# A hybrid HGRN2 / stick-breaking transformer block in float32: the low part of the output projections' moving operand by a subtraction on VectorE, and the feed-forward's sums moved from GpSimd to VectorE

## The chip, the cores and the metric

One core of one Trainium2 chip runs the whole block as one launch. The metric is device microseconds of that core. The kernel before took 2149.41 us, the median of 3 runs (2149.28 to 2149.68). The engines are called by the names of the profile: PE is TensorE (PEld its weight loads), DVE is VectorE, ACT is ScalarE, POOL is GpSimd, SP is SyncE, which here only issues DMAs.

## What is computed

A transformer block of depth 1 on a sequence of 1024 tokens and a width of 1024, in float32. The parts that this change touches are the three output projections and the feed-forward. Cut to what matters:

```python
y_hg = o_hg @ w_hg_out                         # 1024 x 1024 @ 1024 x 1024
y_sb = o_sb @ w_sb_out
mixed = sigmoid(ga) * y_hg + sigmoid(gb) * y_sb
x = x + mixed @ w_o
h2 = rms_norm(x, norm2_gain)
gate, up = split_cols(h2 @ w_ffn_in, (2816, 2816))
x = x + (silu(gate) * up) @ w_ffn_out
```

Ahead of them lie a norm, the input projections, the HGRN2 mixer and the stick-breaking attention. They fill about the first 1200 us of the span.

## The kernel before

**Numbers in two parts.** TensorE multiplies a rounded form of float32 (`F32R`). To keep float32 accuracy, each operand is split into a high part, `hi`, which is the operand rounded to `F32R`, and a low part, `lo = raw - hi`. A product is three matmuls into one PSUM bank: hi*hi, hi*lo and lo*hi (`mm3`, L140 to L144). So each operand costs, besides its load, a cast on ACT (`hi`) and a subtraction (`lo`).

There are two helpers for the low part. `split` (L875 to L877) casts on ACT at L876 and subtracts on an engine that is handed to it, at L877. `rest_by_dma` (L106 to L109) instead lets ACT write the negated high part into `lo` (L107), and then lets POOL issue a DMA that adds `raw` to it on the way (L108, `accum_op=add`).

**Seven products for eight.** The three output projections, and the two products of the feed-forward, use a scheme of seven block products `m` = 1 to 7 in place of the eight of a 2 x 2 partition (four quarters of A, four of B). Some of the seven take a sum or difference of quarters as an operand; `sum_step` (L870 to L873) makes it in place in the raw tiles. The quarters have the numbers 11, 12, 21 and 22. The products are summed in four PSUM banks per chain, and partial results are taken out after each product.

**Output projections** (`Product`, L887 to L943). A phase is one projection, of seven jobs, one for each `m`; there are 21 jobs, `job_steps(0)` to `job_steps(20)`. A job is 4 tiles of 4 steps of 3 matmuls of 128 x 512, 48 in all. While it runs, `prep` of the job after it is woven in, in four parts: `moving(0)`, `moving(1)`, `stationary(0)` and `stationary(1)`. The stationary side is summed by `sum_step` at L873 and split by `split`, on DVE, in two halves of 1024 elements a partition. The moving side is summed on DVE, cast on ACT (L925), and its low part comes by `rest_by_dma` (L926), also in two halves of 1024 elements. The raw quarters of the job two ahead are loaded on SP.

After each tile, partial results leave PSUM: `accumulate` copies them on ACT (L953) or adds them on DVE (L951). Where a result is final, `gated` loads the gate's values from DRAM into one of three `m` tiles (L977, SP), takes the sigmoid on ACT (L978) and multiplies on DVE (L979); in the second phase DVE also adds the first phase's result (L986). In the third phase DVE adds each tile to `x` (L991).

**Feed-forward in.** The last job of the projections is woven with `turn_h2`, which multiplies by the norm (L1068, DVE), transposes on PE (L1072), and splits the moving operands `bop[1]`, `[2]`, `[5]`, `[6]` and `[7]` piece by piece (`b_op`, on DVE). The operands for `m` = 3 and 4 are made later by `b_rest` (L1098), four pieces of 128 x 512 each, and these go through `rest_by_dma`. Then 22 column blocks `f` follow, each of seven units of 12 matmuls (`ffn_step`). Their order is the list `a_order`; `a_prep(n)` (L1123 on) makes the stationary operand of the unit `n`, up to five units ahead of the matmuls. For n up to 22 its sum and its subtraction are on DVE. For later ones the sum is on POOL, and so is the subtraction of `m` = 5, 6, 7 and 3; those of `m` = 1, 2 and 4 are on DVE. DVE also takes the results out (L1192, L1171, L1178, L1180).

**Feed-forward out.** Seven products of 11 groups of 12 matmuls (`ffn_out`); `o_tile` makes both operands of a group, up to three groups ahead, on DVE. While `m` = 1 and 2 run, POOL makes the sums that the moving operand of `m` = 5 and 7 will need, 22 of 128 x 512.

**What sets the order.** PE's order is that of the code. On the other engines the tile framework places the instructions by its own estimate of time, so they do not stand in the order of the code. Each engine then runs its instructions strictly in turn, and so does SP's queue of DMA issues; each instruction waits for the ones that it depends on, and those behind it wait too.

Of the kernel before, what the change touches and what calls it, by code (L numbers as in the profile page):

```python
# [34 lines left out]
def hybrid_block(ctx, tc, x, norm1_gain, w_in, lb_logits, hg_out_norm, sb_q_norm, sb_k_norm,  # L35
                 w_hg_out, w_sb_out, w_o, norm2_gain, w_ffn_in, w_ffn_out,
                 c_ident, c_blk, c_lvl, c_base, out):
    nc = tc.nc
# [848 lines left out]
    class Product:  # L887
# [17 lines left out]
        def prep(self, i):  # L905
            m = self.seq[i]
            sides = self.ops[i] = [], []

            def stationary(c):
                cols = slice(c * 256, (c + 1) * 256)  # L910
                raw = lambda q: self.raw("a", q)[:, :, cols]
                hi = wp.tile([P, 4, 256], F32R, tag="wh", name="wh")
                lo = wp.tile([P, 4, 256], F32R, tag="wl", name="wl")
                sides[0].append((hi, lo))
                sum_step(self.a_sum, A_STEPS, m, raw)
                split(nc.vector, raw(A_SRC[m]), hi, lo)

            def moving(c):
                if c == 0:
                    sides[1].extend((unit1(), unit1()))  # L920
                ks = slice(2 * c, 2 * c + 2)
                raw = lambda q: self.raw("b", q)[:, ks, :]
                sum_step(nc.vector, B_STEPS, m, raw)
                hi, lo = (u[:, ks, :] for u in sides[1])
                nc.scalar.copy(hi, raw(B_SRC[m]))  # L925
                rest_by_dma(lo, raw(B_SRC[m]))  # L926
            return [lambda: moving(0), lambda: moving(1), lambda: stationary(0), lambda: stationary(1)]

        def tile(self, i, j):
# [153 lines left out]
    bop = {}  # L1083

    def b_op(m, cut, e):
# [2 lines left out]
            bop[m] = [unit() for _ in range(2)]  # L1088
        raw = lambda q: h2f[q][cut]
        sum_step(e, B_STEPS, m, raw)  # L1090
        if cut[2:]:
            split(e, raw(B_SRC[m]), *(u[cut] for u in bop[m]))
        else:
            hi, lo = (u[cut] for u in bop[m])
            nc.scalar.copy(hi, raw(B_SRC[m]))
            rest_by_dma(lo, raw(B_SRC[m]))

    def b_rest(m, e):  # L1098
        for q in range(4):
# [23 lines left out]
    def a_prep(n):  # L1123
# [4 lines left out]
            load_raw(f + 1)  # L1128
        raw = lambda q: raws[f][q // 10 - 1][:, 4 * (q % 10) - 4:4 * (q % 10), :]
        both = wp.tile([P, 2, 4, P], F32R, tag=("wh", "wl")[n % 2], name="wh")  # L1130
        sum_step(nc.gpsimd if n > 22 else nc.vector, A_STEPS, m, raw)
        split(nc.vector if m in (1, 2, 4) or n <= 22 else nc.gpsimd, raw(A_SRC[m]), both[:, 0], both[:, 1])
        a_ops[f, m] = both

    a_done = []
# [79 lines left out]
    def o_tile(m, g):  # L1215
        def load():
# [7 lines left out]
            split(nc.vector, A(A_SRC[m]), hi[:, 0], lo[:, 0])  # L1224
            split(nc.vector, B(B_SRC[m]), hi[:, 1], lo[:, 1])
            if m in (1, 2):
                sum_step(nc.gpsimd, B_STEPS, {1: 5, 2: 7}[m], B)
            return hi, lo
        return load

# [111 lines left out]
```

## Time and profile before

| | |
|---|---|
| median of 3 runs | 2149.41 us (2149.28 to 2149.68) |
| the profiled execution's own time | 2149.9 us |
| its span, first to last instruction | 2148.1 us |
| mean granted TensorE clock | 0.989 |
| busy in the span: PE, DVE, ACT, POOL | 95%, 63%, 53%, 26% |
| output projections, first matmul of job 0 to first of job 20 | 1213.4 to 1473.5 us, 260.1 us |
| job 20 woven with the transposes, and the start of the feed-forward | 1473.5 to 1552.3 us, 78.8 us |
| feed-forward in, the steady part | 1552.3 to 1920.3 us, 368.0 us |
| feed-forward out | 1920.3 to 2148.1 us, 227.8 us |

In the profile's rows a line number is that of the kernel, `out<-in` are tile names without their buffer numbers, and the shape is partitions x elements. `u` is the name of all large tiles of these stages, raw or split; `wh` and `wl` are the high and low parts of the stationary side; `wr` are raw weights; `pd`, `pt`, `pz` and `po` are PSUM banks. In a row of idle time, `<-` names the engine and line that ended the wait.

### The profile page before, as it was taken

How to read it: one execution, taken by the hardware profiler on the slowest of the kernel's cores; microseconds unless marked ns; L12 is line 12 of the kernel's file. 1: busy time of each engine (PE TensorE's matmuls, PEld its weight loads, DVE VectorE, ACT ScalarE, POOL GpSimd, SP SyncE). 2: the span in 40 equal slices, each digit the busy share in tenths (PEclk: the TensorE clock that was granted, in tenths of full speed). 3: DMA queues.
4: the chain of work that ended last, by engine and by line, in shares of the span. 5: the costliest groups of instructions: out<-in, count | busy, mean ns of one | idle time of the engine just before them, and what ended most of it. 6: DMA issues, size and time to landing. Idle time of an engine off the chain costs nothing.

```text
span 2148.1 us, 29624 instructions
## 1 busy us (share of the span) xinstructions
PE 2045.9 (95%) x10981; PEld 1730.3 (81%) x10981; DVE 1364.0 (63%) x2130; ACT 1143.5 (53%) x1879; POOL 559.0 (26%) x610
## 2 busy tenths in 40 slices
PE   7999999999999999999999998989899999999999
PEld 6889898988877877877887776767688888887887
DVE  6475757656387787788778356678733333337965
ACT  4454554453476776767767365666533333333443
POOL 4333323232221122022020011110255555545000
PEclk9999999999999999999999999999999999999999
DMA  4433334335534434344343779982512322255221
GB/s 147 110 87 94 94 81 115 74 97 135 134 86 105 95 89 115 83 103 103 84 112 101 242 190 263 252 171 99 127 60 79 103 79 75 63 180 210 76 101 46
DMA packets 203840, 250.47 MB, mean 117 GB/s; under 512 B 11256, under 2 KB 134576, under 8 KB 203696
## 3 DMA queue, kind: packets, MB, share of 16 engines
q1 hardware_dynamic: 179552, 183.43, 27.4%
q0 software_dynamic: 16848, 59.25, 14.7%
q10 hardware_dynamic: 7296, 5.90, 0.8%
q8 instruction: 86, 1.41, 0.3%
q14 instruction: 58, 0.48, 0.1%
HBM read 134.51 MB, written 38.01 MB: 80 GB/s over the span
## 4 chain that ended last, share of the span: by engine, by line
PE 67%; DVE 15%; DMA 7%; ACT 6%; issue 4%; POOL 0%; SPq 0%; DVEq 0%; ACTq 0%; POOLq 0%
PE pd L142 15%; PE pd L143 15%; PE pd L144 15%; DVE kp L737 3%; PE pt L144 2%; PE pt L142 2%; PE pt L143 2%; PE pt L770 2%; DMA u<-u 2%; DVE a L744 2%; DVE wl L877 1%; PE pz L507 1%; PE po L142 1%; PE po L787 1%; PE po L144 1%
## 5 line engine op out<-in xcount | busy, mean ns | idle before, releaser
L142 PE MATMUL pd<-hT,wh 128*128 128x512 f32 (+1 forms) x920 | 375.9, 409 | 0.0
L143 PE MATMUL pd<-hT,wh 128*128 128x512 f32 (+1 forms) x920 | 356.4, 387 | 0.5 <-DVE hT L192 0.5
L144 PE MATMUL pd<-hT,wl 128*128 128x512 f32 (+1 forms) x920 | 356.4, 387 | 0.0
L876 ACT CAST wh<-u 128x512 fp32r<-128x512 f32 (+1 forms) x280 | 183.6, 684 | 224.5 <-PE po L144 70.5
L877 DVE TENSOR_TENSOR wl<-u,wh 128x512 fp32r<-128x512 f32 (+1 forms) x196 | 164.1, 873 | 85.0 <-ACT wh L876 82.8
L143 PE MATMUL pd<-u,wh 128*128 128x512 f32 x496 | 197.5, 398 | 12.7 <-DMA u<-u 10.5
L142 PE MATMUL pd<-u,wh 128*128 128x512 f32 x496 | 198.0, 399 | 10.3 <-ACT wh L876 5.5
L144 PEld LDWEIGHTS pd<-hT,wl 128*128 128x128 f32 x920 | 174.2, 189 | 36.3
L143 PEld LDWEIGHTS pd<-hT,wh 128*128 128x128 f32 x920 | 175.5, 191 | 21.4 <-DVE hT L192 0.8
L142 PEld LDWEIGHTS pd<-hT,wh 128*128 128x128 f32 x920 | 175.4, 191 | 21.1
L737 DVE TENSOR_TENSOR_SCAN kp<-kp,dsel 128x512 f32<-128x512 f32 (+3 forms) x128 | 129.5, 1012 | 39.9 <-ACT kp L730 39.9
L142 PE MATMUL pd<-wh,hT 128*128 128x256 f32 x512 | 148.0, 289 | 0.0
L730 ACT ACTIVATE kp<-pz,rq 128x128 f32<-128x128 f32 (+2 forms) x192 | 112.9, 588 | 61.3 <-PE pz L726 52.7
L144 PE MATMUL pd<-wh,hT 128*128 128x256 f32 x512 | 144.8, 283 | 0.0
L143 PE MATMUL pd<-wl,hT 128*128 128x256 f32 x512 | 144.7, 283 | 0.0
L108 POOL DMA_DIRECT2D wl<-wr x67 | 59.0, 880 | 312.6 <-ACT wl L107 240.6
L144 PE MATMUL pd<-u,wh 128*128 128x512 f32 x352 | 138.4, 393 | 0.0
L873 DVE TENSOR_TENSOR u<-u,u 128x512 f32<-128x512 f32 (+1 forms) x130 | 110.3, 883 | 42.7 <-DMA u<-u 13.1
L143 PEld LDWEIGHTS pd<-u,wh 128*128 128x128 f32 x496 | 95.4, 192 | 35.7 <-issue 6.3
L142 PEld LDWEIGHTS pd<-u,wh 128*128 128x128 f32 x496 | 95.4, 192 | 31.7 <-ACT wh L876 6.4
L744 DVE TENSOR_TENSOR a<-a,kp 128x128 f32<-128x128 f32 (+2 forms) x192 | 109.5, 571 | 14.0
L730 ACT ACTIVATE a<-pz,rq 128x128 f32<-128x128 f32 (+2 forms) x192 | 112.8, 587 | 2.7 <-PE pt L770 2.7
(270 smaller groups left out, 5036.7 us busy)
## 6 DMA issues: line engine op xcount, KB each, us to landing
wr<-in_w_in SPq DMA_DIRECT2D x72, 512.0 KB, 3.7
wl<-wr POOLq DMA_DIRECT2D x67, 512.0 KB, 4.6
u<-u POOLq DMA_DIRECT2D x42, 512.0 KB, 7.4
u<-in_w_ffn_in SPq DMA_DIRECT2D x24, 512.0 KB, 5.2
wr<-in_w_ffn_in SPq DMA_DIRECT2D x20, 512.0 KB, 3.7
u<-in_w_ffn_out SPq DMA_DIRECT2D x10, 1024.0 KB, 5.1
d_act<-c SPq DMA_DIRECT2D x33, 256.0 KB, 2.1
u<-d_act SPq DMA_DIRECT2D x8, 1024.0 KB
```

The lines of the kernel that those rows point to most:

```text
L108: nc.gpsimd.dma_start(lo.bitcast(F32).rearrange("p k n -> p (k n)"), raw.rearrange("p k n -> p (k n)"), accum_op=ALU.add)
L142: nc.tensor.matmul(ps, lh, rh, start=start, stop=False, skip_group_check=adds)
L143: nc.tensor.matmul(ps, lh, rl, start=False, stop=False, skip_group_check=adds)
L144: nc.tensor.matmul(ps, ll, rh, start=False, stop=stop, skip_group_check=adds)
L507: nc.tensor.matmul(ps[:, sl], kq[:, 0, sl], kq[:, 1, sl], start=True, stop=True)
L730: last["sig"] = [nc.scalar.activation(t[:, 0:w], ps[:, 0:w], AF.Sigmoid, scale=rq[:, n_, col:col + 1]) for n_, t in enumerate((kp, a))]
L737: nc.vector.tensor_tensor_scan(rev, rev, dsel[:, HS - w:][:, ::-1], initial=0.0, op0=ALU.mult, op1=ALU.max)
L744: nc.vector.tensor_mul(a[:, 0:w], a[:, 0:w], kp[:, 1:w + 1])
L770: nc.tensor.transpose(tp[:, s * P:(s + 1) * P], a[:, b * P:(b + 1) * P], ident)
L873: e.tensor_tensor(raw(to), raw(a), raw(b), op=op)
L876: nc.scalar.copy(hi, src)
L877: e.tensor_sub(lo, src, hi.bitcast(F32))
```

## The change

```diff
 # Product.prep, moving(c): output projections
                 hi, lo = (u[:, ks, :] for u in sides[1])
-                nc.scalar.copy(hi, raw(B_SRC[m]))
-                rest_by_dma(lo, raw(B_SRC[m]))
+                split(nc.vector, raw(B_SRC[m]), hi, lo)
 # b_op: moving operands of the feed-forward
-        if cut[2:]:
-            split(e, raw(B_SRC[m]), *(u[cut] for u in bop[m]))
-        else:
-            hi, lo = (u[cut] for u in bop[m])
-            nc.scalar.copy(hi, raw(B_SRC[m]))
-            rest_by_dma(lo, raw(B_SRC[m]))
+        split(e, raw(B_SRC[m]), *(u[cut] for u in bop[m]))
 # a_prep: stationary operands of the feed-forward
-        sum_step(nc.gpsimd if n > 22 else nc.vector, A_STEPS, m, raw)
-        split(nc.vector if m in (1, 2, 4) or n <= 22 else nc.gpsimd, raw(A_SRC[m]), both[:, 0], both[:, 1])
+        sum_step(nc.vector, A_STEPS, m, raw)
+        split(nc.vector, raw(A_SRC[m]), both[:, 0], both[:, 1])
 # o_tile: second product of the feed-forward
             if m in (1, 2):
-                sum_step(nc.gpsimd, B_STEPS, {1: 5, 2: 7}[m], B)
+                sum_step(nc.vector, B_STEPS, {1: 5, 2: 7}[m], B)
```

In the output projections, 42 negations on ACT and 42 adding DMAs that POOL issues (512 KB each) become 42 subtractions on DVE (128 x 1024). The same happens to 8 pieces of 128 x 512 of the feed-forward's moving operand. In the feed-forward 76 sums and 76 subtractions of 128 x 512 move from POOL to DVE in the first product, and 22 sums in the second. The arithmetic is the same, and so is PE's order of work. The input projections, ahead of all this, go on using `rest_by_dma`.

Since the framework places the work of DVE, ACT and POOL, the order there changes. Two places are shown.

The first is DVE at the start of the first projection. `u1_12221`, `u1_12367` and `u1_12449` (after: `u1_12221`, `u1_12365`, `u1_12445`) are the raw quarters 11, 12 and 22 of the moving side, `wl_12416` (after `wl_12412`) is a low part of the stationary side of job 1. Before:

```order
L873 TENSOR_TENSOR u1_12221<-u1_12367,u1_12221 128x1024 [waits DMAHW5_49,DMAHW4_49,DMAHW7_49,DMAHW0_49,DMASW4_49]
L877 TENSOR_TENSOR wl_12416<-u1_12249,wh_12415 128x1024 [waits DMASW7_49,DMAHW7_49,PE_49,Activation_49]
L873 TENSOR_TENSOR u1_12372<-u1_12372,u1_12374 128x4x256 [waits DMAHW7_49,DMAHW6_49]
L873 TENSOR_TENSOR u1_12372<-u1_12372,u1_12374 128x4x256
L873 TENSOR_TENSOR u1_12367<-u1_12449,u1_12367 128x1024 [waits DMAHW2_49,DMAHW1_49,DVE_49]
L877 TENSOR_TENSOR wl_12433<-u1_12249,wh_12432 128x1024 [waits PE_49,Activation_49]
L873 TENSOR_TENSOR u1_12367<-u1_12449,u1_12367 128x1024 [waits DMAHW4_49,DMAHW3_49,DVE_49]
L951 TENSOR_TENSOR u2_12397<-u2_12397,pt_12460 128x512 [waits PE_49]
```

And after (L950 is the L951 of before):

```order
L873 TENSOR_TENSOR u1_12221<-u1_12365,u1_12221 128x1024 [waits DMAHW5_49,DMAHW4_49,DVE_49]
L877 TENSOR_TENSOR wl_12412<-u1_12247,wh_12411 128x1024 [waits DMASW7_49,DMAHW7_49,PE_49,Activation_49]
L877 TENSOR_TENSOR u1_12375<-u1_12242,u1_12374 128x1024 [waits DMAHW3_49,Activation_49]
L877 TENSOR_TENSOR u1_12375<-u1_12242,u1_12374 128x1024 [waits DMAHW6_49,Activation_49]
L873 TENSOR_TENSOR u1_12370<-u1_12370,u1_12372 128x4x256 [waits DMAHW7_49,DMAHW6_49]
L877 TENSOR_TENSOR wl_12429<-u1_12247,wh_12428 128x1024 [waits PE_49,Activation_49]
L873 TENSOR_TENSOR u1_12370<-u1_12370,u1_12372 128x4x256
L873 TENSOR_TENSOR u1_12365<-u1_12445,u1_12365 128x1024 [waits DMAHW2_49,DMAHW1_49,DVE_49]
L873 TENSOR_TENSOR u1_12365<-u1_12445,u1_12365 128x1024 [waits DMAHW4_49,DMAHW3_49,DVE_49]
L877 TENSOR_TENSOR u1_12451<-u1_12221,u1_12450 128x1024 [waits PE_49,Activation_49]
L873 TENSOR_TENSOR u1_12221<-u1_12445,u1_12221 128x1024 [waits DVE_49]
L950 TENSOR_TENSOR u2_12394<-u2_12394,pt_12455 128x512 [waits PE_49]
```

What moved: the subtractions of the moving side (`u1_12375` for job 1, `u1_12451` for job 2) now stand among the sums and the stationary side's subtractions, and the first sum no longer waits for an adding DMA (DMASW4).

The second place is the start of the feed-forward's steady part. Before, POOL has there the last of `b_rest`'s adding DMAs (`u2_14568`, for `m` = 4), then the sums for `m` = 5 of the column blocks 4, 5, 7 and 9 (`wr_14714`, `u1_14851`, `u1_15119`, `u1_15387`), each of which waits for its block's load, and behind them the work on block 3 (`u1_14287`):

```order
L873 TENSOR_TENSOR wr_14714<-wr_14714 128x512 [waits DMAHW5_49]
L108 DMA u2_14568<-u1_14115 128x512 [waits DMASW2_49,DVE_49,Activation_49]
L108 DMA u2_14568<-u1_14115 128x512 [waits DMASW3_49,DVE_49,Activation_49]
L108 DMA u2_14568<-u1_14115 128x512 [waits DMASW4_49,DVE_49,Activation_49]
L873 TENSOR_TENSOR u1_14851<-u1_14851 128x512 [waits DMASW6_49,DMASW7_49,DMASW5_49,DMAHW7_49,DMASW0_49,PE_49]
L873 TENSOR_TENSOR u1_15119<-u1_15119 128x512 [waits DMAHW1_49]
L873 TENSOR_TENSOR u1_15387<-u1_15387 128x512 [waits DMASW4_49,DMASW3_49,DMAHW3_49,DMASW2_49,DMASW1_49]
L877 TENSOR_TENSOR wh_14773<-u1_14287,wh_14773 128x512 [waits DVE_49,PE_49,Activation_49]
```

After, the same sums stand on DVE (blocks 4, 5, 7 and 9 are now `wr_14664`, `u1_14801`, `u1_15069` and `u1_15337`), and the first result of column block 1 to leave PSUM (L1186, the L1192 of before) stands behind them:

```order
L877 TENSOR_TENSOR wh_14628<-u1_14245,wh_14628 128x512 [waits DMAHW6_49,PE_49,Activation_49]
L873 TENSOR_TENSOR u2_14236<-u2_14236 128x512
L873 TENSOR_TENSOR wr_14664<-wr_14664 128x512 [waits DMAHW6_49]
L873 TENSOR_TENSOR u1_14801<-u1_14801 128x512 [waits DMAHW7_49]
L877 TENSOR_TENSOR wh_14646<-u2_14236,wh_14646 128x512 [waits PE_49,Activation_49]
L873 TENSOR_TENSOR u1_15069<-u1_15069 128x512 [waits DMAHW1_49]
L873 TENSOR_TENSOR u1_15337<-u1_15337 128x512 [waits DMAHW3_49]
L1186 TENSOR_TENSOR c_14552<-c_14552,pd_14349 128x512 [waits PE_49]
```

What moved: four sums that wait for loads, and on which nothing close by depends, have come from POOL's queue into DVE's, between the split of a unit and the taking out of a result.

## The prediction

> **What bounds the kernel now.** I read the page first, then the busy times by stage, then what PE waited for in the stages that the change touches, then DVE, ACT, POOL and the DMA queues there.
>
> ```profile
> span 2148.1 us, 29624 instructions
> PE 2045.9 (95%) x10981; PEld 1730.3 (81%) x10981; DVE 1364.0 (63%) x2130; ACT 1143.5 (53%) x1879; POOL 559.0 (26%) x610
> ```
>
> The 63% of DVE is an average. By stage (length, then busy time and instructions of PE, PEld, DVE, ACT and POOL, granted clock, DMA share, GB/s): output projections, their join to the feed-forward, feed-forward in, feed-forward out; and the projections again from 1231 us on.
>
> ```profile
> 1213.40:1473.50 260.10, 232.31 (x962) 186.41 (x961) 165.92 (x196) 155.70 (x204) 34.68 (x40) 0.94 0.79 210
> 1473.50:1552.30 78.80, 67.37 (x303) 53.57 (x302) 63.58 (x121) 52.18 (x108) 14.70 (x13) 0.91 0.52 136
> 1552.30:1920.30 368.00, 368.00 (x1624) 304.51 (x1622) 134.81 (x196) 136.98 (x231) 195.72 (x148) 1.00 0.27 86
> 1920.30:2148.10 227.80, 219.98 (x961) 179.50 (x960) 169.66 (x251) 87.57 (x154) 32.62 (x22) 1.00 0.33 115
> 1231.00:1473.50 242.50, 218.51 (x905) 175.63 (x905) 159.54 (x191) 147.88 (x194) 32.95 (x38) 0.94 0.77 200
> ```
>
> Feed-forward in is PE alone: 1624 matmuls in 368.00 us, with no idle time, 0.2266 us each. That is the pace of an unhindered PE. The 20 jobs of the projections, 960 matmuls, would take 217.5 us at it and took 260.1, so 42.6 us are lost there: 27.8 of idle time (260.10 - 232.31), and 14.8 of slower matmuls. These follow the gaps:
>
> ```profile
> 1258.76 0.59 PE L143 MATMUL pd<-u,wh 128*128 128x512 f32 x1 [3.56 <-DMA u<-u]
> 1259.15 0.63 PE L144 MATMUL pd<-u,wl 128*128 128x512 f32 x1
> 1259.57 0.63 PE L142 MATMUL pd<-u,wh 128*128 128x512 f32 x1
> ```
>
> After a gap of 3.56 us matmuls start every 0.42 us. PE waits for several things, of which the adding DMAs (`u<-u`) are the largest group; first the projections, then the join:
>
> ```profile
> PE pd L142 <- ACT wh L876: 5.5, 2, 4.7
> PE pd L143 <- DMA u<-u: 5.1, 2, 3.6
> PE pt L143 <- DMA u<-u: 4.1, 3, 2.3
> ...
> PE pd L143 <- DMA u<-u: 5.4, 3, 3.8
> PE pt L1072 <- DVE hn L1068: 3.8, 1, 3.8
> ```
>
> What lies behind the rest is seen in the DMA queues of the projections (packets, MB, share of 16 engines), and in ACT:
>
> ```profile
> q0 software_dynamic: 5760, 20.97, 42.0%
> q1 hardware_dynamic: 19152, 33.16, 36.8%
> u<-u POOLq DMA_DIRECT2D x40, 512.0 KB, 7.2
> ...
> L107 ACT ACTIVATE u<-u 128x1024 fp32r<-128x1024 f32 x40 | 42.1, 1058 | 0.0
> L978 ACT ACTIVATE m<-m 128x512 f32<-128x512 f32 x32 | 19.6, 629 | 60.2 <-DMA m<-d_ga 30.8 <-DMA m<-d_gb 29.3
> ```
>
> The adding DMAs take 42.0% of the DMA engines, more than all plain loads and stores (36.8%), and land 7.2 us after issue. ACT waits 60.2 us for gate tiles on those same engines, and with it the casts queued behind.
>
> **The change, part by part.** First the price of a subtraction on DVE, from runs of the same instruction back to back:
>
> ```profile
> 1252.90 5.76 DVE L873 TENSOR_TENSOR u<-u,u 128x1024 f32<-128x1024 f32 x5
> 1517.56 2.50 DVE L877 TENSOR_TENSOR u<-u,u 128x512 fp32r<-128x512 f32 x4
> ```
>
> So 1.15 us for 1024 elements, 0.625 for 512.
>
> *Projections.* Removed in this stage: 40 negations (42.1 us of ACT), 40 issues on POOL and 42.0% of the DMA engines. A moving low part used to come 1.06 us of ACT plus 7.2 us of DMA after the cast; it will come one DVE slot after it. Added: 40 subtractions on DVE. Two of them fall ahead of 1231 us, where DVE mostly waits for the first loads (`d_ohg`, `in_w_hg_out` below); I leave those waits as they are. From 1231 us on DVE has 159.5 us of work and gets 38 x 1.15 = 43.7 more: 203.2. Without a wait it would be through at 1434.2, 39.3 us sooner than 1473.5. PE needs the sum of 217.5 us from 1213.4, 1430.9. So the two engines come out alike, and what counts is which of DVE's waits stay:
>
> ```profile
> DVE wl L877 <- ACT wh L876: 32.7, 14, 4.9
> DVE u L979 <- ACT m L978: 13.1, 3, 5.8
> DVE u L873 <- DMA u<-u: 13.1, 4, 4.8
> DVE u L873 <- DMA u<-d_ohg: 12.0, 3, 9.3
> DVE u L873 <- DMA u<-in_w_ffn_in: 7.6, 1, 7.6
> DVE u L873 <- DMA u<-in_w_hg_out: 6.0, 1, 6.0
> DVE u L873 <- DMA u<-d_osb: 5.5, 2, 3.2
> ```
>
> The 13.1 for `u<-u` go. The waits for ACT, gate tiles and other loads (32.7 + 13.1 + 7.6 + 5.5 = 58.9) shrink, since ACT loses 42 of 156 us and the DMA engines over half their load; by how much no row shows. Bounds: none stays (gain 39.3); all stay, which is a rival below. I take a quarter, 15 us, nearer to none, because a DVE that runs late finds its casts done. Gain 39.3 - 15 = 24.3. Queued behind a late DVE are the results that free PSUM banks (L951, L991) and the gate multiplications that free the `m` tiles, so PE does feel it.
>
> Of the Trainium skill, Trace Analysis, section Optimizing Scalar/DVE Operations, speaks against this edit: with a saturated DVE, some work may go to Scalar or GPSIMD, and here it comes back. No run so far shows DVE saturated for long; what it would give is the third rival.
>
> *Join.* Eight subtractions of 512 come to DVE (8 x 0.625 = 5.0), and up to five of POOL's sums (3.1): 63.6 + 8.1 = 71.7 of 78.8 us. PE's 5.4 us of waits for the adding DMAs go, with slow matmuls behind them. So 7.1 is the most that DVE allows; if it delays the transposes' inputs as now (3.8), the gain could be lost or turn to -3. I take 5.
>
> *Feed-forward in.* 152 instructions move; POOL needs 195.72 us for 148 of them in this stage, DVE 148 x 0.625 = 92.5. DVE goes from 134.8 to 227.3 of 368 us, 62%. It now idles ahead of each result:
>
> ```profile
> 1709.39 0.69 DVE L877 TENSOR_TENSOR wh<-wr,wh 128x512 fp32r<-128x512 f32 x1 [3.23 <-ACT wh L876]
> 1716.36 0.69 DVE L1192 TENSOR_TENSOR c<-c,pd 128x512 f32<-128x512 f32 x1 [6.28 <-PE pd L144]
> ```
>
> A unit is 12 x 0.2266 = 2.72 us, and operands are made up to five units ahead, 13.6 us. I cost this at nothing, up or down: PE has nothing to gain. The cover goes if a sum on DVE waits for its load for longer than the two units (5.4 us) after which PE returns to the same bank. POOL's queue has such waits, harmless there:
>
> ```profile
> 1540.37 1.28 POOL L873 TENSOR_TENSOR u<-u 128x512 f32<-128x512 f32 x1 [5.32 <-DMA u<-in_w_ffn_in]
> ```
>
> *Feed-forward out.* Twenty-two sums move. While POOL made them, DVE's own instructions were slow, and PE waited:
>
> ```profile
> 1943.79 20.23 DVE L877 TENSOR_TENSOR wl<-u,wh 128x512 fp32r<-128x512 f32 x12 [1.42 <-ACT wh L876]
> ...
> 1941.85 26.30 POOL L873 TENSOR_TENSOR u<-u,u 128x512 f32<-128x512 f32 x16 [0.70 <-DMA u<-in_w_ffn_out]
> ...
> 1968.75 0.50 PE L143 MATMUL pt<-wl,wh 128*128 128x512 f32 x1 [1.66 <-DVE wl L877]
> 1955.00:1975.00 20.00, 17.24 (x72) 12.99 (x71) 17.40 (x18) 6.56 (x13) 12.91 (x8) 1.00 0.21 67
> ```
>
> Twelve splits took 1.69 us each beside POOL, against 0.625 alone. With the sums on DVE two splits and one or two sums make 1.9 to 2.5 us per group of 2.72. In the last row 72 matmuls stand where 88 fit, 3.6 us lost. I take 3 back, between 0 and 4.5. The Trainium skill, SBUF — State Buffer, section Who interferes with whom, says that DVE and GpSimd lock one another out of a shared port pair; the trace agrees, 12 x (0.625 + 1.28) = 23 against 20.23 us.
>
> *Sum.* 24.3 + 5 + 0 + 3 = 32.3. The profiled execution's own time is 2149.9, 1.8 over its span and 0.5 over the median of 2149.41. Taken from the median, 2117.
>
> **The rivals.** *PE sets the pace throughout* (0.12): no wait of DVE stays, 39.3 + 7.1 + 4.5 = 50.9, 2098.5. For it: the DMA share halves. Against: DVE then has no idle microsecond for 200 us, and it depends on ACT at every split.
>
> *DVE becomes the bound, and most waits stay* (0.16): 35 of 58.9, gain 4 in the projections and 2 each in join and output: 2141. For it: 32.7 us are handshakes with ACT, which an engine that works in turn meets at each new subtraction too.
>
> *DVE carries all its waits along* (0.07), the slower end: after 1231 us it idles 242.5 - 159.5 = 83.0; less 13.1, 69.9 stay. Then 1231 + 203.2 + 69.9 = 1504.1, 30.6 later than now, 2180. It decides from 39.3 us of remaining waits. Against: many of those waits are for DMAs that shared the engines with the transfers removed, or for PE, which is late itself.
>
> *Waits of the hoisted sums stop DVE in the feed-forward* (0.05): two waits like POOL's 5.32 cost PE up to 10.6, so 2128 with the rest as forecast. Against: these loads start earlier when no adding DMA holds their buffers.
>
> That the change does nothing has no room: the DMAs are gone from the queue.
>
> **How the numbers follow.** The forecast, 2117, has 0.60; with waits of 3 to 28 us it spans 2105 to 2130. The range from 2097 to 2139 takes in the first and last rivals and leaves out most of the second and all of the third. A difference of 0.2%, 4.3 us, is about what a measurement of this kernel can tell from none. Slower: 0.07, the third rival. Same: 0.03, the second rival's edge. Faster: 0.90.
>
> **What would show it.** Right: no L107 or L108 row on `u`, and the 20.97 MB of q0 in the projections gone; the stretch of jobs 0 to 19 some 24 us shorter, with DVE over 85% busy in it; DMA share near 0.4, and ACT's wait for `m` well under 60.2; feed-forward in still 0.2266 us a matmul; the splits beside the sums of the second product at 0.6 to 0.7 us. Wrong: a gain without a DVE near its limit (first rival), PE waits for DVE in the place of those for DMAs that sum to 25 us or more (second and third), or a DVE L873 that waits for `in_w_ffn_in` with PE idle behind it (fourth).

## The result

The changed kernel takes 2092.7 us (median of 4 runs, 2091.42 to 2094.44) against 2149.35 us before (4 runs, 2143.7 to 2149.68): ratio 0.9743, 95% interval 0.9725 to 0.9761. That is faster by 57 us. Of all the executions below, two ran at a granted clock of 0.56 and 0.66 and took 3362 and 2878 us, one with a late low part and one with VectorE past its limit, and the ratios leave them out. The forecast was 2117 with a range from 2097 to 2139, so the sign was right and the size was not: 32 us were forecast, and the time lies 4 us below the range. The profile of the changed kernel, its page's first lines:

```profile
span 2091.1 us, 29348 instructions
PE 2026.5 (97%) x10981; PEld 1723.8 (82%) x10981; DVE 1508.6 (72%) x2354; ACT 1103.1 (53%) x1829; POOL 280.3 (13%) x386
```

The busy times by stage, in the columns of the prediction: output projections, join, feed-forward in, feed-forward out.

```profile
1212.40:1430.00 217.60, 217.60 (x961) 180.24 (x960) 206.63 (x236) 122.06 (x165) 0.00 (x0) 1.00 0.42 146
1430.00:1500.60 70.60, 64.60 (x304) 52.96 (x303) 69.12 (x133) 48.61 (x100) 0.00 (x0) 0.95 0.40 121
1500.60:1868.60 368.00, 367.77 (x1623) 304.20 (x1621) 230.75 (x344) 135.25 (x232) 0.00 (x0) 1.00 0.27 86
1868.60:2091.10 222.50, 218.42 (x960) 179.90 (x960) 168.61 (x272) 87.46 (x154) 0.00 (x0) 1.00 0.33 118
```

In the projections PE is busy for the whole of 217.60 us at full clock, with VectorE at 95%. What VectorE and ScalarE still wait for there, and the DMA queue (us in total, times, longest; packets, MB, share):

```profile
DVE u L877 <- ACT u L876: 3.2, 5, 1.4
DVE wl L877 <- ACT wh L876: 2.5, 5, 0.9
DVE u L873 <- DMA u<-d_osb: 2.0, 1, 2.0
...
ACT m L977 <- DMA m<-d_gb: 20.5, 10, 3.9
...
ACT m L977 <- DMA m<-d_ga: 13.8, 8, 3.4
...
q1 hardware_dynamic: 18080, 31.18, 41.6%
```

PE has no wait at all in this stretch. VectorE's 32.7 us for `wh` have become 2.5, the 13.1 for gate tiles are gone, and ScalarE's 60.2 us for gate tiles are 34.3.

To compare kernels, the table below takes the times between the same matmuls of the program, counted from the first of the output projections: number 0, 960 (the last job), 1008 (the feed-forward's first), 1164 (its unit 13), and the first of the second product. Each row is of one profiled execution.

| kernel | median us | jobs 0 to 19 | job 20 | units 0 to 12 | units 13 on | second product |
|---|---|---|---|---|---|---|
| before | 2149.35 | 260.1 | 14.6 | 56.7 | 384.5 | 218.8 |
| changed | 2092.7 | 217.6 | 14.6 | 48.2 | 384.5 | 213.8 |

The difference is 42.5 + 0 + 8.5 + 0 + 5.0, and 1.0 in front of the projections, which the change doesn't touch: 57.0 us of span. Every job of the twenty takes 10.88 us now.

### The profile page after: what moved, and what is told of

It is laid out like the page before. It is cut to its first block, busy times and chain, and to the rows that moved or that the text cites. A ratio compares the mean times of both kernels' runs of the same rounds, so it can differ in the third digit from the quotient of the medians.

```text
span 2091.1 us, 29348 instructions
## 1 busy us (share of the span) xinstructions
PE 2026.5 (97%) x10981; PEld 1723.8 (82%) x10981; DVE 1508.6 (72%) x2354; ACT 1103.1 (53%) x1829; POOL 280.3 (13%) x386
## 4 chain that ended last, share of the span: by engine, by line
PE 75%; DVE 17%; ACT 5%; issue 3%; DMA 1%; DVEq 0%; ACTq 0%
PE pd L142 16%; PE pd L143 16%; PE pd L144 16%; PE pt L143 3%; PE pt L144 3%; PE pt L142 3%; DVE kp L737 3%; PE pt L770 2%; DVE u L873 2%; DVE u L877 2%; PE po L142 2%; PE po L143 2%; PE po L144 2%; DVE a L744 1%; PE pz L507 1%
## 5 line engine op out<-in xcount | busy, mean ns | idle before, releaser
L876 ACT CAST wh<-u 128x512 fp32r<-128x512 f32 (+1 forms) x280 | 183.7, 685 | 231.2 <-PE po L144 86.6
L142 PE MATMUL pd<-u,wh 128*128 128x512 f32 x496 | 193.9, 391 | 1.2 <-ACT c L1184 0.7
L143 PE MATMUL pd<-u,wh 128*128 128x512 f32 x496 | 193.1, 389 | 0.0
L877 DVE TENSOR_TENSOR wl<-u,wh 128x512 fp32r<-128x512 f32 (+1 forms) x196 | 150.3, 799 | 46.2 <-ACT wh L876 44.1
L144 PE MATMUL pd<-u,wh 128*128 128x512 f32 x352 | 137.0, 389 | 0.0
L873 DVE TENSOR_TENSOR u<-u,u 128x512 f32<-128x512 f32 (+1 forms) x152 | 124.4, 851 | 9.0 <-DMA u<-d_ohg 4.4
L773 DVE TENSOR_TENSOR tl<-pt,th 128x512 fp32r<-128x512 f32 (+1 forms) x160 | 99.3, 625 | 20.8 <-ACT th L772 20.8
L770 PE MATMUL pt<-ident,a 128*128 128x128 f32 x576 | 90.4, 277 | 23.2 <-DVE a L744 14.6
L772 ACT CAST th<-pt 128x512 fp32r<-128x512 f32 (+1 forms) x160 | 86.7, 546 | 46.9 <-PE pt L770 41.6
```

Of the source, the lines that this page charges most:

```text
L142: nc.tensor.matmul(ps, lh, rh, start=start, stop=False, skip_group_check=adds)
L143: nc.tensor.matmul(ps, lh, rl, start=False, stop=False, skip_group_check=adds)
L144: nc.tensor.matmul(ps, ll, rh, start=False, stop=stop, skip_group_check=adds)
L770: nc.tensor.transpose(tp[:, s * P:(s + 1) * P], a[:, b * P:(b + 1) * P], ident)
L772: nc.scalar.copy(th[:, c0:], tp[:, c0:])
L773: nc.vector.tensor_sub(tl[:, c0:], tp[:, c0:], th[:, c0:].bitcast(F32))
```

## Experiments: the parts alone

Each of four kernels is the one before with one hunk of the diff. Their medians stand against runs of the kernel before on the same chip (2148.4 us, 25 runs from 2144.28 to 2153.78).

**The projections alone** (the hunk in `moving`).

> Before, with only the edit of the output projections (moving low part by subtraction on VectorE). Theory A (the adding DMAs of this stage, and what waits behind them, are the whole loss there): every job from the second on takes 10.88 us, the stage gains 42.5 us as in the changed kernel, and the join gains next to nothing since its own eight adding DMAs stay: 2104 to 2109. Rival B (the adding DMAs of the stage delay the loads of the join, or the join pays for work that was put off): 2097 to 2103, with the join shorter too. Rival C (GpSimd's work anywhere slows VectorE, so that only the edits together bring it): 2115 or more, with jobs over 10.88 us.

Measured: 2105.4, ratio 0.9805 (0.979 to 0.9819). Jobs 0 to 19 take 217.6 us, the units 0 to 12 take 55.8. Theory A holds: the whole gain of the stage comes from this hunk, with GpSimd's other work as before.

**The operands for `m` = 3 and 4 alone** (the hunk in `b_op`).

> Before, with only the edit of the operands for m = 3 and 4, whose low parts come by subtraction on VectorE. Theory A: the 5.4 us of PE's waits for adding DMAs in the join go, with the slow matmuls behind them, and the rest is as before: 2140 to 2144. Rival B (the join lost time to what the projections left behind): 2146 to 2149.5, no change that can be told. A third way: VectorE is full in the join (60.8 of 71.3 us busy), eight subtractions more put off the multiplications by the norm, and it is 2150 to 2153.

Measured: 2144.25, ratio 0.9982 (0.9973 to 0.9992); units 0 to 12 take 54.4 in the place of 56.7. PE's waits for adding DMAs are gone there, though one of 4.1 us for a cast has come up, and the median is 4 us lower, just past the edge of theory A's range and below rival B's.

**The first product alone** (the hunk in `a_prep`).

> Before, with only the edit of the feed-forward's first product: its sums and subtractions all on VectorE. Theory A: matmuls stay at 0.2266 us each there, GpSimd was hidden, no change: 2148 to 2150.5. Rival C (GpSimd slows VectorE's instructions where both work): a gain of 1 to 4 us, in the last units of the join, where VectorE is busy: 2145 to 2148. A third way: VectorE takes on three or four sums more in the join and is 1 to 3 us late there: 2151 to 2153.

Measured: 2144.8, ratio 0.9986 (0.9972 to 1.0). Its units from 13 on take 384.49 us as before; the units 0 to 12 take 55.4, 1.3 less, and most of the rest of the difference lies ahead of the edited lines. The measurement shows that this part isn't slower; it can't tell a small gain from none.

**The second product alone** (the hunk in `o_tile`).

> Before, with only the edit of the second product: the 22 sums for m = 5 and 7 on VectorE. Theory A (VectorE's splits took 1.69 us beside GpSimd's sums, and PE waited): the stage takes 216.5 us and the whole gain of 5.0 us of the changed kernel comes from here: 2143.5 to 2145.5. Rival (part of the 5.0 us is the gap ahead of the stage, or comes from earlier loads): under 3 us, 2146.5 to 2149.

Measured: 2143.6, ratio 0.9979 (0.9969 to 0.999); the stage takes 213.8 us, 5.0 less than before, as in the changed kernel. Theory A. VectorE's groups in that stage, before and after:

```profile
L877 DVE TENSOR_TENSOR wl<-u,wh 128x512 fp32r<-128x512 f32 x150 | 110.3, 780 | 38.4 <-ACT wh L876 38.4
L873 DVE TENSOR_TENSOR u<-u,u 128x512 f32<-128x512 f32 x66 | 42.4, 685 | 6.1 <-DMA u<-d_act 6.1
```

```profile
L877 DVE TENSOR_TENSOR wl<-u,wh 128x512 fp32r<-128x512 f32 x150 | 96.7, 686 | 39.1 <-ACT wh L876 39.1
L873 DVE TENSOR_TENSOR u<-u,u 128x512 f32<-128x512 f32 x87 | 55.9, 683 | 2.2 <-DMA u<-d_act 2.0
```

VectorE took on 21 sums, 13.5 us, and lost 13.6 us from the subtractions that used to run beside GpSimd. Its busy time is the same, and the sums are no longer GpSimd's to wait for.

The four parts give 43.0 + 4.2 + 3.6 + 4.8 = 55.6 us together, the change 55.7 from the same 2148.4. That they add up so closely is in part luck: the gains in the stages that were edited, 42.5 + 4.5 + 5.0 = 52.0, fall 4 us short, and most of what the first product's part gained lies ahead of its lines.

## Experiments: what the adding DMA cost in the projections

Before the change an adding DMA did three things at once: ScalarE negated for it, its transfer took DMA time, and its result came late. The kernels below put one of these back into the changed kernel, load VectorE further, or put the whole DMA back. The edits of the first five:

```diff
 act_kept:      hi, lo = (u[:, ks, :] for u in sides[1])
-               split(nc.vector, raw(B_SRC[m]), hi, lo)
+               nc.scalar.copy(hi, raw(B_SRC[m]))
+               nc.scalar.activation(lo, raw(B_SRC[m]), AF.Copy, scale=-1.0)
+               nc.vector.tensor_sub(lo, raw(B_SRC[m]), hi.bitcast(F32))
 latency_kept:  (behind the split)
+               nc.gpsimd.dma_start(t, lo[:, :, 0:16].bitcast(F32))
+               nc.gpsimd.dma_start(lo[:, :, 0:16].bitcast(F32), t)
 dve_plus:      (behind the split)
+               if c == 0:
+                   nc.vector.tensor_sub(lo, raw(B_SRC[m]), hi.bitcast(F32))
 load_kept:     (behind the split; scr and d_ga in DRAM)
+               nc.gpsimd.dma_start(scr[n % 2], d_ga[n % 8], accum_op=ALU.add)
 load_behind:   (the same, but it reads the low part just made)
+               nc.gpsimd.dma_start(scr[n % 2], lo..., accum_op=ALU.add)
```

**ScalarE's negations back.**

> The changed kernel, and ScalarE also writes the negation of each moving half into the low part, as before the change, ahead of VectorE's subtraction that overwrites it: ScalarE's 42 us of negations are back in the projections, the adding DMAs are not. Theory L (a low part that comes 8 us after its cast) and theory Q (adding DMAs that take 42% of the DMA engines from the loads): ScalarE has 122 us of work in 217.6 and takes 42 more beside it, jobs stay at 10.88 us, 2091 to 2096. Theory K (ScalarE's queue: casts for VectorE came late behind negations): 15 us or more come back, 2107 to 2130.

Measured: 2094.4, ratio 0.976 (0.9745 to 0.9775). Jobs 0 to 19:

```profile
1211.42:1430.00 218.58, 217.92 (x962) 180.10 (x960) 205.93 (x236) 156.59 (x205) 0.00 (x0) 1.00 0.43 145
```

ScalarE is as busy as before the change (156.6 against 155.7) and the stage loses 1.0 us. Theory K falls.

**A late low part.**

> The changed kernel, in which 16 columns of each low half (16 KB) go out to DRAM and back on GpSimd's queue after VectorE's subtraction: the operand is ready some 5 us later as with the adding DMA, and there is next to no load on the DMA engines. Theory L (latency): the first matmuls of a job with the low part wait, 10 to 40 us come back, 2103 to 2135. Theory Q (load): an operand made about a job (10.88 us) ahead hides 5 us, jobs stay at 10.88 us, 2091 to 2096.

Measured: 2096.6, ratio 0.9768 (0.9752 to 0.9785). The two transfers land 3.0 and 2.8 us after issue, PE waits for them in two early jobs (12.59 and 13.90 us in the place of 10.88), and the stage takes 222.3:

```profile
scr<-u POOLq DMA_DIRECT2D x40, 16.0 KB, 3.0
u<-scr POOLq DMA_DIRECT2D x39, 16.0 KB, 2.8
...
PE pd L146 <- DMA u<-scr: 2.4, 2, 1.4
PE pt L146 <- DMA u<-scr: 1.4, 1, 1.4
```

So 4.7 us: less than theory L said, and not nothing. The low part is 5.8 us late here; before the change it was 1.06 + 7.2 = 8.3 us late, so 4.7 is rather too little. Even so, a late operand by itself explains a small part of the 42.5 us.

**The load, first attempt.**

> The changed kernel with 42 more adding DMAs of 512 KB, one with each moving half on GpSimd's queue, from one place of DRAM to another that nothing waits for: the load on the DMA engines is back, and no operand waits for it. Theory Q (load): loads of raw quarters and gate tiles come late, PE waits again, 15 to 40 us come back, 2107 to 2135. Theory L (latency of the low part alone): the DMA share rises to 0.7 or so, but jobs stay at 10.88 us, 2091 to 2097.

Measured: 2172.5, ratio 1.0117 (1.01 to 1.0135), slower than before, but it tells nothing on the projections. Nothing held these transfers back, and they were issued long ahead of the projections, which start at 1294.6 us here and take 217.60:

```profile
L930 POOL DMA_DIRECT2D scr<-d_ga x42: 824/845/869, 504.5 to 1110.6; - x42
```

**The load where it was.** Here the transfer reads the low part, so it can't start ahead of it.

> The changed kernel with an adding DMA of 512 KB behind each moving subtraction, which adds the low part just made onto a scratch of DRAM that nothing reads: it can't start ahead of the projections, loads the DMA engines there, and no operand waits for it. Theory Q (load): jobs go over 10.88 us, ScalarE's wait for gate tiles goes up from 34 us, 12 to 40 us come back, 2104 to 2133. Theory L (latency, of which 16 columns out and back brought 4.7 us of the stage's 42.5): 2091 to 2097. If both are needed together (the DMA late because of the load, and PE waiting because the operand is the DMA's): 2091 to 2100.

Measured: 2131.9, ratio 0.9927 (0.991 to 0.9943). Jobs 0 to 19, the waits of VectorE and ScalarE there, and the transfers:

```profile
1211.16:1466.17 255.01, 230.51 (x961) 185.73 (x960) 205.22 (x225) 117.74 (x158) 34.80 (x40) 0.95 0.82 210
```

```profile
DVE u L983 <- ACT m L982: 17.4, 5, 7.9
DVE wl L880 <- ACT wh L879: 16.9, 8, 8.4
...
ACT m L982 <- DMA m<-d_gb: 43.2, 8, 16.8
ACT m L982 <- DMA m<-d_ga: 41.3, 11, 10.4
...
q0 software_dynamic: 5760, 20.97, 45.1%
...
scr<-u POOLq DMA_DIRECT2D x40, 512.0 KB, 7.5
```

No instruction but the next transfer waits for these transfers, so neither a late operand nor a buffer that they hold plays a part. ScalarE has no negations, and still 37.4 of the stage's 42.5 us are back, with 3.8 more in job 20. Theory Q holds: the load on the DMA engines is most of the cost. It is a little heavier here than it was: 45.1% of 258 us is 116 us of the DMA engines, and 42.0% of 260 us was 109. ScalarE waits 84.5 us for gate tiles in the place of 34.3, and VectorE waits for ScalarE again.

**The whole DMA back, with VectorE in ScalarE's place.** In `moving`, VectorE writes the negation and the adding DMA finishes the low part.

> The changed kernel with the adding DMA back in the projections, but VectorE does the negation in ScalarE's place: VectorE's instructions and ScalarE's relief stay as changed, and the DMA's load and latency are as before the change. If the DMA is the whole of the stage's loss: the stage takes 255 us or more again, 2130 to 2140. If ScalarE's 42 us of negations were half of it: 2110 to 2120. If VectorE's load counts on top of the DMA (its queue waits for the DMAs behind which its next sums stand): 2140 to 2160.

Measured: 2137.3, ratio 0.9955 (0.994 to 0.9969); jobs 0 to 19 take 260.25 us, what they took before the change, as the first expectation has it. So close a match is luck: in the three kernels of the parts that leave these lines as before, the jobs took 258.8 to 261.7. Within that, the DMA is the whole loss of the stage, and the 5.2 us over the load alone are what its late operand adds.

**VectorE past its limit.**

> The changed kernel, in which VectorE does the moving subtraction of the first half of each job a second time: 20 x 1.2 = 24 us more in the projections, 206.6 + 24 = 230.6 of busy time where PE needs 217.6. Theory V (VectorE is 11 us short of being the bound, and its remaining waits vanish as it fills): the stage takes 231 to 236 us, 13 to 18 us more, 2105 to 2112. The prediction's third rival (its waits stay and are carried along): 24 us more, 2115 to 2120. If VectorE were no near bound at all (it can run further behind, and catch up in the join): 2092 to 2097.

Measured: 2106.85, ratio 0.9815 (0.9799 to 0.9832). Jobs 0 to 19 take 226.3 (8.7 more), job 20 takes 18.9 (4.3 more): 13.0 us for 24 us of work.

```profile
1212.12:1438.42 226.30, 220.47 (x961) 179.38 (x960) 223.30 (x248) 121.66 (x162) 0.00 (x0) 1.00 0.41 140
```

The whole time is in theory V's range. The stage by itself is under its 231 to 236 us, as a third of the delay fell into job 20, so 206.6 + 24 = 230.6 of work, 13.0 more than PE's 217.6, meets the 13.0 by luck in the last digit; by the medians and the ratios it is 14 to 16 us. In kind theory V holds: VectorE is busy for 223.3 of 226.3 us, the part of the work that fits into PE's time is free, and no waits are carried along.

**The subtraction on GpSimd** (`split(nc.gpsimd, ...)` in `moving`).

> The changed kernel with the moving subtractions of the projections on GpSimd: some 2.5 us each, 100 us in all, and VectorE's work there back to 166 us. If the removed DMA is the gain, it stays whichever engine subtracts: 2091 to 2097, and with VectorE no longer near its limit. If GpSimd slows VectorE while it works, as beside the sums of the second product (1.69 us for a split that takes 0.63): 40 x 1.2 = 48 us land on VectorE all the same, and it is 2091 to 2100 too, but VectorE's busy time stays over 200 us. If an operand that is 1.3 us later counts: 2096 to 2105.

Measured: 2139.2, ratio 0.9962 (0.9947 to 0.9977). All three expectations of the time were wrong (the second was right that VectorE stays over 200 us): jobs 0 to 19 take 260.9 us, though no adding DMA runs and the DMA share is 0.36. GpSimd's group, and VectorE's beside it:

```profile
1211.61:1472.50 260.89, 231.26 (x962) 184.81 (x960) 207.94 (x195) 119.50 (x165) 135.51 (x40) 0.95 0.36 122
...
L877 POOL TENSOR_TENSOR u<-u,u 128x1024 fp32r<-128x1024 f32 x40 | 135.5, 3411 | 114.2 <-ACT u L876 105.5 <-DVE u L873 6.9 <-issue 1.7
...
L877 DVE TENSOR_TENSOR wl<-u,wh 128x1024 fp32r<-128x1024 f32 x40 | 67.6, 1691 | 35.7 <-ACT wh L876 35.7
L985 DVE TENSOR_TENSOR u<-u,u 128x512 f32<-128x512 f32 x16 | 15.3, 957 | 0.1
L990 DVE TENSOR_TENSOR u<-u,pd 128x512 f32<-128x512 f32 x9 | 6.0, 679 | 0.2 <-PE pd L144 0.2
```

The same three groups of VectorE in the changed kernel:

```profile
L877 DVE TENSOR_TENSOR wl<-u,wh 128x1024 fp32r<-128x1024 f32 x40 | 48.6, 1216 | 2.5 <-ACT wh L876 2.5
...
L985 DVE TENSOR_TENSOR u<-u,u 128x512 f32<-128x512 f32 x16 | 10.9, 684 | 0.1
L990 DVE TENSOR_TENSOR u<-u,pd 128x512 f32<-128x512 f32 x9 | 6.1, 674 | 0.0
```

VectorE does 40 instructions fewer and is busy for 207.9 us in the place of 206.6. Its groups with two operands in SBUF take 1.4 times as long, while the one that reads a PSUM bank takes 0.68 us in both. The Trainium skill, SBUF — State Buffer, section Who interferes with whom, says that a DVE instruction with two SBUF inputs contends with a GpSimd instruction that reads SBUF, and one with at most one SBUF input, outside the 2-port modes, does not: these rows agree. So GpSimd took nothing off VectorE, the operand came some 3.4 us after its cast (the mean; the median is 2.9), and ScalarE's casts and VectorE met more waits (35.7 us for `wh`). ScalarE waits 57.5 us for gate tiles, too, nearly the 60.2 of before the change, at less than half of the DMA share of then:

```profile
ACT m L977 <- DMA m<-d_gb: 29.2, 8, 10.5
ACT m L977 <- DMA m<-d_ga: 28.3, 11, 6.4
```

SyncE waits 87.7 us there for VectorE's multiplications before it issues these loads (73.7 in the changed kernel), so a late VectorE makes them late, too. Long waits for gate tiles are therefore no proof of full DMA engines; it is the run with the transfers put back that shows their part in the kernel before. What each of these waits cost PE wasn't taken apart.

## Experiments: by which way the load reached PE

My next theory was that the load reaches PE through the gate tiles: ScalarE waits for one ahead of its casts. The following three kernels leave out the sigmoid, or sigmoid and gate; each was executed once.

```diff
 gated:  g = mp.tile(...); nc.sync.dma_start(g, ...)
-        last["gate"] = nc.scalar.activation(g, g, AF.Sigmoid)
+        last["gate"] = nc.scalar.activation(<a tile of 1 column>, eps, AF.Sigmoid)
-        nc.vector.tensor_mul(y, g, of)        (no sigmoid: this line stays)
+        nc.vector.tensor_mul(y, y, y)         (free gates; a PSUM bank times 0.5)
```

> The changed kernel with an adding DMA behind each moving subtraction, as before, and the sigmoid of the gates left out: VectorE multiplies by the gate tile as it was loaded, so ScalarE's queue never waits for a gate tile and VectorE waits in its place. If the load reaches PE through ScalarE's in-order queue (casts behind sigmoids that wait for late gate tiles): the stage goes from 255 us to 218 to 232. If any in-order queue that meets the late gate tiles has the same effect: 235 to 255, with VectorE's waits for gate tiles in place of ScalarE's. If it is the raw quarters: 250 to 258.

> The same with the gate tiles still loaded, but nothing reads them: sigmoid and gate are left out, VectorE squares or halves the result in place of the multiplication. If the late gate tiles are the way by which the load reaches PE: 218 to 225 us in the stage. If it is the raw quarters of the next jobs: 245 to 255.

> The kernel before the change, with gate tiles that are loaded and not read, as in the run above. If the gate tiles are the way, the stage goes from 260 us to what the later low part and ScalarE's negations cost by themselves, 217.6 + 4.7 + 1.0 = 223 or so, up to 230. If the raw quarters and the operands are: 245 to 260.

Measured: 2138.0, 2151.7 and 2156.7. These times can't be compared as a whole: with the small sigmoid, ScalarE loads its tables anew between logarithm and exponential in job 20, which takes 27 to 31 us:

```profile
L1007 ACT ACT_TABLE_LOAD x6 | 7.7, 1283 | 0.1
```

Jobs 0 to 19 end ahead of that: 239.9 us without the sigmoid and 251.0 with free gates, against 255.0 for the load behind; 250.5 with free gates against 260.1 before. Without the sigmoid the stage comes nowhere near the 218 to 232 of a load that reaches PE through ScalarE's wait alone: 15 of 37 us go, and VectorE now waits for the gate tiles itself, so the second expectation fits: any queue that works in order meets the late tiles. Its waits without the sigmoid:

```profile
DVE u L983 <- DMA m<-d_ga: 14.9, 4, 6.4
...
DVE u L983 <- DMA m<-d_gb: 7.7, 4, 3.2
```

With free gates nothing waits for these tiles, and a raw quarter of a later job is late instead. But SyncE's queue has changed, too: here are the wait and the issues with free gates, and then the first issues of the same quarters with the load behind.

```profile
ACT u L879 <- DMA u<-d_osb: 28.3, 2, 28.0
...
1226.89 32.78 SPq L981 DMA_DIRECT2D m<-d_ga  x14
1259.97 27.57 SPq L981 DMA_DIRECT2D m<-d_gb  x16
...
1288.06 15.52 SPq L967 DMA_DIRECT2D u<-d_osb  x12
```

```profile
1262.64 5.12 SPq L967 DMA_DIRECT2D u<-d_osb  x8
```

As gate loads no longer wait for VectorE's multiplications, 30 of them stand in one row in front of the raw quarters, which go out some 20 us later from the stage's start. One job alone, the one with this wait, takes 34.6 us: 24 of the 33 us that the stage loses. The kernel before with free gates has the same order and a wait of 23.0 us for a quarter. So these two kernels lose most of their time to an order that their own edit made, and they can't tell whether the load would reach PE without the gate tiles.

What is left: ScalarE's wait for gate tiles is a part of the way, some 15 of 37 us in the one run that removes it alone, and the rest of the way isn't known.

What the kernels with the load have in common is the amount of DMA work. The stage in thirds, before (length; PE, PEld, DVE, ACT, POOL; clock, DMA share, GB/s) and after:

```profile
1213.40:1300.00 86.60, 76.97 (x315) 61.08 (x313) 43.62 (x45) 54.84 (x68) 13.00 (x15) 0.94 0.84 222
1300.00:1390.00 90.00, 82.22 (x346) 66.85 (x347) 61.50 (x72) 55.61 (x73) 11.26 (x13) 0.94 0.90 261
1390.00:1473.50 83.50, 73.11 (x303) 58.48 (x302) 60.80 (x80) 45.25 (x65) 10.41 (x12) 0.94 0.63 142
```

```profile
1212.40:1285.00 72.60, 72.60 (x322) 60.13 (x321) 67.12 (x70) 44.97 (x58) 0.00 (x0) 1.00 0.56 195
1285.00:1357.50 72.50, 72.50 (x322) 60.05 (x321) 67.85 (x76) 41.71 (x54) 0.00 (x0) 1.00 0.49 172
1357.50:1430.00 72.50, 72.50 (x321) 60.07 (x320) 71.66 (x91) 35.39 (x54) 0.00 (x0) 1.00 0.22 70
```

Before, the DMA engines were busy for 0.84 x 86.6 + 0.90 x 90.0 = 154 us in the first two thirds, more than the 145 us that PE needs for two thirds of the stage, and twice the 0.56 x 72.6 + 0.49 x 72.5 = 76 us of now. Half of the load tells whether it bounds by amount alone (`load_behind` with the transfer only for `c == 0`):

> The changed kernel with an adding DMA behind the first moving half of each job alone: 20 in the place of 40. The DMA engines then have about 91 + 57 = 148 us of work in the stage where PE needs 217.6, and some 61 us in its fullest third of 72.5. If the load bounds by its amount: the stage takes 217.6 to 223 us, 2091 to 2098. If each transfer costs its share of the 37 us: 18 us or so come back, 2107 to 2116.

Measured: 2105.45, ratio 0.9801 (0.9785 to 0.9818). Jobs 0 to 19 take 226.15, 8.5 more than without a load, and job 20 takes 18.8, 4.2 more. Its thirds from 1212 us on have shares of 0.81, 0.72 and 0.46:

```profile
1212.00:1295.00 83.00, 81.42 (x358) 66.71 (x358) 71.21 (x73) 45.10 (x59) 6.96 (x8) 1.00 0.81 242
```

So neither: half of the transfers cost 23% of the 37.4 us in the stage, 31% with job 20. The cost grows faster than the load, but it begins before the DMA engines are full, since single loads come late in front of queues that work in order (20.5 us for `m<-d_gb` became 32.7).

## Experiments: what bounds the join now

PE has one wait of more than a microsecond in the join, with slow matmuls behind it, and VectorE is busy for 47.5 of the 48.2 us of units 0 to 12:

```profile
PE pt L1071 <- DVE hn L1067: 5.5, 1, 5.5
...
1444.60:1492.85 48.25, 42.25 (x189) 34.38 (x188) 47.52 (x85) 31.19 (x60) 0.00 (x0) 0.93 0.36 101
```

Three kernels try to take work off VectorE there or to order it otherwise: operands made two units ahead at first (`a_ahead(n + min(6, 2 + max(0, n - 4) // 3))`); the norm's factor and gain on ScalarE, four pieces of 128 columns per transpose; the sums and subtractions for `m` = 5, 6 and 7 one turn later, and operands two units ahead up to unit 14.

> The changed kernel, in which the stationary operands of the feed-forward are made two units ahead in the first seven units and only later up to five ahead: VectorE's queue in the join (47.5 of 48.2 us busy) loses four or five operands of 1.9 us. If VectorE bounds the join, as the one wait of PE for the multiplication by the norm (5.5 us, and 2.5 us of slow matmuls behind it) says: 2084 to 2089. If the order of the units is what bounds it: no change, 2091 to 2094. If operands made only two units ahead come late: 2095 to 2102.

> The changed kernel, in which the feed-forward's norm does not run on VectorE: ScalarE multiplies by the row's factor, and the gain is multiplied in as ScalarE takes the transposes out (four pieces of 128 columns, as the gain then lies along the partitions). VectorE loses 16 x 0.66 = 10.6 us around the join, ScalarE gains 16 x 0.6 and 48 short instructions. If the amount of VectorE's work bounds the join (62.7 of 63 us busy) and PE's 5.5 us wait for the multiplication is its sign: the units 0 to 12 take 40 to 44 us in the place of 48.2, 2084 to 2089. If it is the chain through transposes, ScalarE and the sums, whichever engine multiplies: 2091 to 2096. If ScalarE is too full: 2096 to 2102.

> The changed kernel, in which the sums and subtractions for m = 5, 6 and 7 come one turn later than the transposes they belong to, so that the multiplication by the norm of the next turn does not stand behind them on VectorE, and the stationary operands are made two units ahead up to unit 14 and then slowly further. If PE's wait in the join (5.5 us, and 2.5 us of slow matmuls) is a matter of order: 2084 to 2089. If VectorE's amount of work bounds the join: four operands fewer are 3 to 4 us, 2088 to 2090. If neither: 2091 to 2096, with the wait in another place.

Measured: 2093.5 (ratio 0.975, 0.9736 to 0.9765), 2102.8 (0.979, 0.9771 to 0.9808) and 2095.0 (0.9755, 0.974 to 0.9769). None beats the changed kernel. The first left VectorE as busy (47.0 us, one instruction fewer): its operands had caught up by unit 12, so it doesn't test the idea. The second moved PE's wait to ScalarE, and job 20 took 21.5 us in the place of 14.6:

```profile
PE pt L1068 <- ACT hn L1065: 9.1, 3, 4.6
```

ScalarE is busy for 20.2 of these 21.5 us, and the units 0 to 12 take 51.7 us, not 40 to 44: the third expectation, a ScalarE that is too full, fits.

The third has its wait in the same place (5.7 us in two pieces) and units 0 to 12 take 51.1. That VectorE's amount of work bounds the join fits its 47.5 of 48.2 us, but no run has shown it.

## Why the prediction was wrong

- **Where the missing time lies.** The spans differ by 57.0 us where 32.3 were forecast. Of the 24.7 us between, 18.2 are the projections (42.5 for 24.3), 3.5 the join, 2.0 the second product, and 1.0 lies ahead of all edited lines. The 18.2 are the 15 us of waits below and 3.2 us of a bound that was too small.
- **The bound of the projections.** Right in kind: with the adding DMAs gone, VectorE's work of 203 us from 1231 on (190.5 measured up to 1430, as some of it lies ahead) and PE's 217.5 come out alike. Too small in size: 39.3 as the most that could be gained left the waits ahead of 1231 us as they were, and they went too. The whole 42.6 us that the text itself counts as lost was there to be had, and 42.5 came.
- **The step that failed: "I take a quarter, 15 us, nearer to none".** Of the 58.9 us of VectorE's waits some 8 stay, and PE feels none. I took these waits as separate risks of an engine that works in turn. Most of them went with one cause: DMA engines at 0.84 and 0.90 in the two fullest thirds, where my row of the whole stage showed 0.79. With nothing but the transfers put back, VectorE waits again for the casts (16.9 us) and the gates (17.4). The load alone costs 37.4 of 42.5 us, the late operand 4.7 and ScalarE's negations 1.0 when each is put back. My text named all three and credited ScalarE's 42 of 156 us as much as the DMA. By which queue the load reached PE stays open beyond ScalarE's wait for gate tiles.
- **The first rival was what happened**, PE setting the pace throughout, with a chance of 0.12. What spoke against it, a VectorE without an idle microsecond that depends on ScalarE at every split, does not hold: at 206.6 of 217.6 us it lost nothing. Its price, 2098.5, was 6 us too slow, for the bounds of all three terms were too small. Its sign, a gain without a VectorE near its limit, didn't come: VectorE is busy for 95% of the stage, and PE sets the pace all the same. The other signs that the forecast gave for being right did come (no adding DMA, a DMA share of 0.42, 34.3 us of waits for gate tiles, splits of 0.69 us), but for the size of the gain, so they could not tell the forecast from this rival.
- **Second and third rival.** Most waits went, so neither came. The extra subtractions exclude the third once more: 24 us of work cost 13.0, so waits aren't carried along.
- **Join.** 5 forecast, 7.1 the most; 8.5 in the profiles. The parts' runs share it out as 0.9, 2.3 and 1.3 us, some 4.5 together, and the same units took 58.8 us in the kernel with the second product alone, which doesn't touch them, against 56.7. So the size of this term is known to some 2 us only.
- **Feed-forward in.** Right: 384.49 us from unit 13 on in both, no wait of PE, VectorE at 230.75 of 368 us where 227.3 was said. The fourth rival's waits for loads come to 4.6 us in front of VectorE's sums, and PE feels none.
- **Feed-forward out.** Right in mechanism, the splits take 0.69 us; 3 was forecast and 5.0 came, 0.5 over the bound, because I counted the lost matmuls of one stretch of 20 us. The working 12 x (0.625 + 1.28) = 23 is not met as well as I wrote: 20.23 is 12% under it. The rows show that the two engines hinder one another, not that only one of them works at a time.
- **The page against the edit.** The Trainium skill, Perfetto Trace Analysis, section Optimizing Scalar/DVE Operations, also says that moving work between DVE and GpSimd might not help. The subtraction on GpSimd agrees, 2139.2 against 2092.7. It is no rule for every stage, though: in the feed-forward's first product GpSimd's 148 instructions did spare VectorE work, which is busy for 134.81 us there before the change and for 230.75 after, and PE has no idle time to speak of in either.

## What to carry to other kernels

Look for one cause behind many waits before discounting them one by one, and read the DMA share by thirds of a stage: here 0.81, 0.72 and 0.46 already cost PE 8.5 us of the stage, and 0.84, 0.90 and 0.63 came with the loss of 42.5. The waits themselves don't name the cause. Queues that work in order pass any delay on, and a subtraction that was slow on GpSimd made much the same waits at a share of 0.36, so put one suspect back alone and measure.

Here an engine that works in order ran at 95% of the bounding engine's time without costing it anything, and 24 us of further work cost about what went over that time. Work between two SBUF tiles that was moved from VectorE to GpSimd took nothing off a VectorE that was nearly full, though it did where VectorE was busy for 37% of the stage.

## What the runs showed of the hardware

The adding DMAs took more DMA time by the byte than the plain transfers beside them: 20.97 MB took 42.0% of the 16 engines in the projections before, 33.16 MB of loads and stores 36.8%, so 1.8 times as much. A GpSimd subtraction of 128 x 1024 between SBUF tiles took 3.41 us on average (the median is 2.93) beside a busy VectorE, whose own took 1.22 without it and 1.69 with it, and those with a PSUM operand 0.68 in both. In the feed-forward's first product before the change, GpSimd's instructions of 128 x 512 took 1.3 to 1.4 us, and VectorE's subtractions beside them 0.73; 0.69 after it.
